# The down projection of a hybrid decoder trunk: seven-product steps spread anew, table load moved to its beginning, residual a step later, tail in program order

## The chip, the cores and the metric

The kernel runs on one core of one Trainium2 chip. The metric is the time of one execution on the device in microseconds (us); lower is better. Every kernel is run several times, and the median is what is compared. A profile is one further execution, recorded by the hardware profiler.

The core's engines work side by side, each through its own queue in order: TensorE (PE in the profile; PEld is its loading of the stationary operand), VectorE (DVE), ScalarE (ACT), GpSimd (POOL) and SyncE (SP), which here issues nearly all DMA transfers. Engines wait for each other through semaphores. Matrix products add into PSUM, where VectorE and ScalarE read them.

## The reference, cut to what matters

The model is one layer over 256 tokens with 2048 channels: two token mixers, cross-attention, and a feed-forward part, all in float32. Only the feed-forward part's second matrix and the final norm are touched:

```
def conv_glu_ffn(u, w_up, conv_w, conv_b, w_down):
    gate, up = jnp.split(u @ w_up, 2, axis=-1)
    gate = causal_dwconv(gate, conv_w, conv_b)
    return (jax.nn.gelu(gate, approximate=False) * up) @ w_down
...
        h = h + conv_glu_ffn(u, ffn_w_up[l], ffn_conv_w[l], ffn_conv_b[l], ffn_w_down[l])
    return rms_norm(h, final_norm_g)
```

Here `w_down` is 5632 x 2048, and `rms_norm` divides each token by the root of the mean square of its 2048 channels and multiplies by a gain per channel.

## The kernel before, in words

**Precision.** Products run on float32 rounded to a shorter form (`F32R`). To keep full precision every operand is split into a rounded part `hi` and the remainder `lo`, and a product is made of three: hi x hi, hi x lo, lo x hi (`mm_tok`). ScalarE makes `hi` by a cast, VectorE makes `lo` by a subtraction.

**Weights.** All weight tiles (128 x 2048 floats, 1 MB) stand in one list, `order`, in the order of their use. `weights()` hands out the next one and has up to two more started ahead. `issue()` starts one: a DMA on SP into one of three `raw` buffers (L140), then two casts and two subtractions of 1024 columns (L126, L127). The results lie in a ring of five buffers for `hi` and five for `lo`, freed when the products that read them are done.

**The down projection** (from L899 on) works through the 2048 output channels in two halves, `i` = 0 and 1. A half is four blocks of PSUM, `acc[0]` to `acc[3]`: 128 tokens x 512 channels each, b // 2 the tokens and b % 2 the channels. The 5632 hidden channels are taken in 22 steps of 256. `down_steps` gives their order and says of each whether it is ordinary or one of `NST` = 7 that use Strassen's scheme:

- An ordinary step forms 2 x 2 blocks of output from 2 x 2 blocks of input and weights in eight block products, each made of three: 24 matrix products of 512 columns.
- A seven-product step forms seven products of sums and differences, 21 matrix products, four of which go to PSUM blocks of their own (`own`). For it `seven_forms` (L158 to L169) makes sums of the weight blocks on VectorE, in between four pairs of cast and subtraction: L158, L159, then the sums L164, L165 and L166, two more pairs, the sum L169, and a last pair of 512 columns. It fills four ring buffers. `input_forms(s)` (L905 to L921) makes the sums of the input on VectorE (L910, L914), splits three of them into `xs` (the cast L916 on ScalarE, the remainder L917) and one into the place of an input block that is no longer needed (L919, L920). All tiles named `c` share one buffer.

Before the change the order is, in both halves: two ordinary steps and a seven, six times; one ordinary step and a seven; two ordinary steps. The sevens are thus steps 2, 5, 8, 11, 14, 17 and 19 of 0 to 21. `input_forms(s)` is named at step 3 s of the first half.

**The residual** is added on TensorE: at steps 0, 4, 8 and 12 of each half a tile `hr` of the residual (256 KB, from `h2_d`, L976, one buffer) is loaded and multiplied by the identity into `acc`, in eight products of 128 columns.

**After the last seven of a half** the four `own` blocks are joined into a tile in SBUF (the copy on ScalarE at L989 or L991; VectorE at L992 to L995). In the first half that copy stands in a critical section (L987), together with a load of ScalarE's function table that holds logarithm and exponential (L988); the functions before it were Gelu and copies.

**The end of a half** goes block by block: VectorE adds `acc` to the joined tile (L998), ScalarE squares it and sums along the row (L1000), VectorE multiplies by the gain (L1002; the gain tile `gr` is loaded at L939 at the beginning of each half). In the second half the last two steps, both ordinary, are run block by block, and after a token group's second block its four partial sums are reduced: VectorE adds them (L1006), ScalarE makes the reciprocal root by logarithm and exponential (L266, L267), VectorE and ScalarE scale the token group's channels (L1009, L1012, L1014), and three DMAs write them out (L1011, L1013, L1015).

**What sets the order.** The program is written in Python in one order; a scheduler then places the instructions of every engine's queue by a model of their times, earlier-written ones first where several are ready, and adds the semaphores. So an instruction whose data are there early can stand well ahead of where it is written. `tc.keep_in_program_order` pins an instruction to its written order on its engine, and `tc.tile_critical` keeps a few instructions together as one unit.

Of the kernel before, what the change touches and what calls it, by code (L numbers as in the profile page):

```python
# [9 lines left out]
F32 = mybir.dt.float32  # L10
# [3 lines left out]
AF = mybir.ActivationFunctionType  # L14
# [5 lines left out]
P = 128  # L20
# [29 lines left out]
def down_steps(half):  # L50
    rest = list(range(NST, KF // 2))
    if half:
        rest = rest[-4:] + rest[:-4]
    steps = []
    for s in range(NST):
        steps += [(False, rest.pop(0)) for _ in range(2 if s < NST - 1 else 1)] + [(True, s)]
    return steps + [(False, k) for k in rest]


# [5 lines left out]
def hybrid_trunk(ctx, tc, xT, memT, par, cst, msk, w_k0, w_ka, w_va, w_hg, w_hv, w_ghg, w_bhg, w_dt,  # L65
# [199 lines left out]
    def rsqrt(out, ps, scale, eps_t):  # L265
        S.activation(out=out, in_=ps, func=AF.Ln, bias=eps_t, scale=scale)  # L266
        S.activation(out=out, in_=out, func=AF.Exp, scale=-0.5)  # L267
# [637 lines left out]
    def input_forms(s):  # L905

        k = 2 * s
        tmp = fd.tile([P, 4, 512], F32, name="c")
        a, d = ha[:, k:k + 2, 0:T], ha[:, k:k + 2, T:2 * T]
        V.tensor_tensor(out=tmp[:, 0:2, 0:T], in0=a.bitcast(F32), in1=d.bitcast(F32), op=ALU.add)  # L910
        a11, a21, a12, a22 = [tmp[:, i, j * P:(j + 1) * P] for i in range(2) for j in range(2)]
        y1, x2, x4, y3 = [tmp[:, 2, j * P:(j + 1) * P] for j in range(4)]
        for out, p, q in ((y1, a21, a22), (x2, a11, y1), (x4, a12, x2), (y3, a21, a11)):
            V.tensor_tensor(out=out, in0=p, in1=q, op=ALU.subtract)  # L914
        three = tmp[:, 2, 0:3 * P].rearrange("p (j t) -> p j t", j=3)
        S.copy(out=xs[:, s, :, 0:P], in_=three)  # L916
        V.tensor_tensor(out=xs[:, s, :, P:2 * P], in0=three, in1=xs[:, s, :, 0:P].bitcast(F32),  # L917
                        op=ALU.subtract)
        S.copy(out=ha[:, k, P:T], in_=y3)  # L919
        V.tensor_tensor(out=ha[:, k, T + P:2 * T], in0=y3, in1=ha[:, k, P:T].bitcast(F32),  # L920
                        op=ALU.subtract)  # L921
# [5 lines left out]

    rows = outT.rearrange("(g p) c -> p g c", p=P)
    ss = fd.tile([P, 2, 4], F32, name="ss")
    cs, gr = [], []  # L930
    for i in range(2):
        steps = down_steps(i)
        acc = [pj.tile([P, 512], F32, name="proj") for _ in range(4)]
# [1 line left out]
            + [pm_.tile([P, 512], F32, name="misc") for _ in range(2)]  # L935
        if i:
            acc, own = own, acc
        gr.append(fd.tile([P, 1024], F32, name="gr"))
        nc.sync.dma_start(out=gr[i], in_=fin_g[i:i + 1, :].partition_broadcast(P))  # L939
        for j, (seven, q) in enumerate(steps):  # L940
            last = i == 1 and j >= len(steps) - 2
            if i == 0:
                for s in range(NST):
                    if j == 3 * s:
                        input_forms(s)
            w = weights()
            if last and j < len(steps) - 1:
                held = w, q
# [19 lines left out]
            else:  # L968
                for k in range(2):
                    for b in range(4):  # L970
                        mm_tok(acc[b], inputs(2 * q + k, b // 2), w(2 * k + b % 2, 512),
                               start=j == 0 and k == 0, stop=j == len(steps) - 1 and k == 1)
            if j % 4 == 0 and j < 16:

                hr = fd.tile([P, 2, T], F32, name="hr")
                nc.sync.dma_start(out=hr, in_=h2_d[:, 8 * i + j // 2:8 * i + j // 2 + 2, :])  # L976
# [5 lines left out]
            if seven and q == NST - 1:  # L982
                c = fd.tile([P, 4, 512], F32, name="c") if i == 0 else \
                    big.tile([P, 4, 512], F32, name="h")
                cs.append(c)
                if i == 0:
                    with tc.tile_critical():  # L987
                        nc.scalar.preload_act_table_set("natural_log_exp_and_others")  # L988
                        S.copy(out=c[:, 0, :], in_=own[0])  # L989
                else:  # L990
                    S.copy(out=c[:, 0, :], in_=own[0])  # L991
                V.tensor_tensor(out=c[:, 2, :], in0=own[2], in1=c[:, 0, :], op=ALU.subtract)  # L992
                V.tensor_tensor(out=c[:, 1, :], in0=own[1], in1=c[:, 2, :], op=ALU.add)
                V.tensor_tensor(out=c[:, 2, :], in0=own[3], in1=c[:, 2, :], op=ALU.add)
                V.tensor_tensor(out=c[:, 3, :], in0=own[1], in1=c[:, 2, :], op=ALU.add)  # L995
        for b in range(4):
            g, n = b // 2, b % 2
            V.tensor_tensor(out=c[:, b, :], in0=acc[b], in1=c[:, b, :],  # L998
                            op=ALU.subtract if b == 2 else ALU.add)
            S.activation(out=acc[b], in_=c[:, b, :], func=AF.Square,  # L1000
                         accum_out=ss[:, g, 2 * i + n:2 * i + n + 1])
            V.tensor_tensor(out=c[:, b, :], in0=c[:, b, :], in1=gr[i][:, n * 512:n * 512 + 512],  # L1002
                            op=ALU.mult)
            if i == 1 and n == 1:
                r = fd.tile([P, 2], F32, name="r", bufs=2)
                V.tensor_reduce(out=r[:, 0:1], in_=ss[:, g, :], axis=AX.X, op=ALU.add)  # L1006
                rsqrt(r[:, 1:2], r[:, 0:1], 1.0 / D, eps_t)
                one, two = cs[0][:, 2 * g:2 * g + 2, :], c[:, 2 * g:2 * g + 2, :]
                V.tensor_scalar(out=two[:, 0, :], in0=two[:, 0, :], scalar1=r[:, 1:2], scalar2=None,  # L1009
                                op0=ALU.mult)  # L1010
                nc.sync.dma_start(out=rows[:, g, 1024:1536], in_=two[:, 0, :])  # L1011
                S.activation(out=two[:, 1, :], in_=two[:, 1, :], func=AF.Copy, scale=r[:, 1:2])  # L1012
                nc.scalar.dma_start(out=rows[:, g, 1536:2048], in_=two[:, 1, :])  # L1013
                V.tensor_scalar(out=one, in0=one, scalar1=r[:, 1:2], scalar2=None, op0=ALU.mult)  # L1014
                nc.sync.dma_start(out=rows[:, g, 0:1024].rearrange("p (n c) -> p n c", n=2), in_=one)  # L1015


# [108 lines left out]
```

## Time and profile before

| what | us |
|---|---|
| median of three runs | 2277.38 |
| lowest and highest of them | 2276.11, 2279.4 |
| the profiled execution, its own time | 2275.68 |
| its span, first to last instruction | 2273.9 |
| VectorE busy in the span | 1645.5 |
| ScalarE busy in the span | 1372.4 |

The profile belongs to the execution of 2275.68 us; 1.8 us of it lie outside the span. A row of a view in order of time has the start, the duration, the engine with the line, the operation, the tiles (written <- read), shapes and count, and in brackets the idle time of the engine before it and what ended it. A row of a view by stage has the stage, its length, the busy time of PE, PEld, DVE, ACT and POOL with the number of instructions, the granted TensorE clock, the DMA share and GB/s. In the chain of waits a row has start, length, what, and count. All matrix products carry the line of a helper, L82, so they are told apart by tiles: in the first half `acc` is `proj` and `own` is two `lev` and two `misc`; in the second the two change places.

The down projection lies from about 2024 us to the end of the span. SP's part in it:

```
hr<-h_d SPq DMA_DIRECT2D x8, 256.0 KB, 5.0
gr<-in_fin_g SPq DMA_DIRECT2D x2, 512.0 KB, 3.8
out<-c SPq DMA_DIRECT2D x2, 512.0 KB, 3.2
```

The last number is the median time from issue to landing in us.

### The profile page before, as it was taken

To read this page: it belongs to the slowest core of one execution; us is meant where nothing else is said; L and a number is where in the kernel's file an instruction comes from. 1 tells how busy PE (TensorE), PEld (TensorE's weight loads), DVE (VectorE), ACT (ScalarE), POOL (GpSimd) and SP (SyncE) were. 2 spreads that over 40 slices of the span, in tenths; PEclk is the share of its full clock that TensorE was granted. 3 is DMA by queue.
4 is the path that set the end of the run, shared out by engine and by line. 5 is a ranking of instruction groups with operands and counts; after the bars stand their busy time and mean duration, and the time that the engine had idled before them with its cause. 6 is when DMAs were issued, how large, how long until landed. Compare 5 with 4: busy or idle time off the path is not lost.

```text
span 2273.9 us, 34864 instructions
## 1 busy us (share of the span) xinstructions
PE 2256.7 (99%) x13848; PEld 1964.6 (86%) x13848; DVE 1645.5 (72%) x2718; ACT 1372.4 (60%) x2116; POOL 1.3 (0%) x9
## 2 busy tenths in 40 slices
PE   9999999999999999999999999999999999999998
PEld 8888888888888888888888888888888888888786
DVE  8878879796556677755676755667776777788876
ACT  7566767676446777764556655556555555555544
POOL 0000000000000000000000000000000000000000
PEclk9999999999999999999999999999999999999999
DMA  8645444545555555455565545565555555555563
GB/s 312 236 169 184 167 169 166 182 161 205 186 187 189 187 184 188 168 181 189 186 238 213 199 172 179 178 209 188 190 193 191 185 187 191 194 198 193 196 230 130
DMA packets 70051, 434.90 MB, mean 191 GB/s; under 512 B 7904, under 2 KB 12544, under 8 KB 20864
## 3 DMA queue, kind: packets, MB, share of 16 engines
q1 hardware_dynamic: 69456, 432.09, 53.4%
q8 instruction: 108, 1.77, 0.3%
q10 hardware_dynamic: 432, 0.58, 0.1%
q14 instruction: 55, 0.45, 0.1%
HBM read 426.32 MB, written 6.32 MB: 190 GB/s over the span
## 4 chain that ended last, share of the span: by engine, by line
PE 97%; DVE 1%; ACT 0%; DMA 0%; issue 0%; SPq 0%; DVEq 0%; ACTq 0%
PE proj L82 88%; PE misc L82 5%; PE lev L82 4%; DVE lo L127 0%; DMA raw<-in_w_k 0%; PE lev L686 0%; DVE lo L159 0%; ACT hi L126 0%; DVE e L505 0%; PE lev L802 0%; DVE e L518 0%; ACT L267 0%; ACT L266 0%; DVE s L263 0%; ACT hi L158 0%
## 5 line engine op out<-in xcount | busy, mean ns | idle before, releaser
L82 PE MATMUL proj<-s,hi 128*128 128x512 f32 x4976 | 1196.6, 392 | 2.5 <-ACT hi L343 1.4
L127 DVE TENSOR_TENSOR lo<-raw,hi 128x1024 fp32r<-128x1024 f32 x738 | 884.0, 1222 | 361.9 <-PE proj L82 268.7
L82 PEld LDWEIGHTS proj<-s,hi 128*128 128x128 f32 x4976 | 913.8, 188 | 183.4 <-DVE s L263 2.0
L126 ACT CAST hi<-raw 128x1024 fp32r<-128x1024 f32 x738 | 770.4, 1048 | 421.8 <-PE proj L82 378.9
L82 PEld LDWEIGHTS proj<-s,lo 128*128 128x128 f32 x4976 | 639.5, 191 | 25.0
L82 PE MATMUL proj<-s,lo 128*128 128x256 f32 x4976 | 647.7, 283 | 0.0
L82 PE MATMUL proj<-hi,s 128*128 128x512 f32 x682 | 216.9, 391 | 0.0
L247 ACT COPY jt<-proj 128x256 f32<-128x256 f32 x263 | 97.5, 371 | 152.7 <-PE proj L82 152.0
L82 PEld LDWEIGHTS proj<-hi,s 128*128 128x128 f32 x682 | 127.8, 188 | 26.3
L82 PE MATMUL proj<-lo,s 128*128 128x512 f32 x341 | 132.8, 389 | 0.0
L158 ACT CAST hi<-raw 128x1024 fp32r<-128x1024 f32 (+1 forms) x56 | 51.6, 943 | 80.3 <-DVE raw L166 49.3
L881 DVE SCALAR_TENSOR_TENSOR gc<-g,par_t,gc 128x255 f32<-128x255 f32 x88 | 42.7, 485 | 55.0 <-ACT gc L879 53.4
L159 DVE TENSOR_TENSOR lo<-raw,hi 128x1024 fp32r<-128x1024 f32 (+1 forms) x56 | 60.0, 1090 | 26.6 <-ACT hi L158 26.2
L82 PEld LDWEIGHTS proj<-lo,s 128*128 128x128 f32 x341 | 64.1, 188 | 12.6
L649 DVE SCALAR_TENSOR_TENSOR sz<-t,par_t,sz 128x255 f32<-128x255 f32 (+2 forms) x96 | 46.2, 481 | 19.9 <-ACT sz L646 18.5
L258 DVE SCALAR_TENSOR_TENSOR s<-h,par_t,s 128x256 fp32r<-128x256 f32 x32 | 15.5, 485 | 36.8 <-ACT s L257 36.6
L253 ACT COPY jt<-proj 128x256 f32<-128x256 f32 x32 | 11.9, 372 | 47.0 <-DVE h L252 47.0
L726 ACT ACTIVATE gs<-r 128x256 f32<-128x256 f32 x32 | 13.4, 419 | 39.5 <-DVE r L248 39.5
L82 PE MATMUL proj<-hi,ha 128*128 128x512 f32 x104 | 36.2, 392 | 0.5 <-ACT hi L158 0.5
L518 DVE TENSOR_TENSOR e<-e,kq 128x256 f32<-128x256 f32 x96 | 34.2, 420 | 0.0
L505 DVE TENSOR_TENSOR e<-bb 128x256 f32<-128x256 f32 x96 | 33.6, 421 | 0.4
L82 PE MATMUL lev<-hi,s 128*128 128x512 f32 x92 | 32.7, 390 | 0.0
(287 smaller groups left out, 1759.2 us busy)
## 6 DMA issues: line engine op xcount, KB each, us to landing
raw<-in_w_up SPq DMA_DIRECT2D x88, 1024.0 KB, 4.8
raw<-in_w_hg SPq DMA_DIRECT2D x48, 1024.0 KB, 4.8
raw<-in_w_m SPq DMA_DIRECT2D x48, 1024.0 KB, 4.8
raw<-in_w_dn SPq DMA_DIRECT2D x44, 1024.0 KB, 4.8
raw<-in_w_hv SPq DMA_DIRECT2D x16, 1024.0 KB, 4.8
raw<-in_w_ghg SPq DMA_DIRECT2D x16, 1024.0 KB, 4.8
raw<-in_w_bhg SPq DMA_DIRECT2D x16, 1024.0 KB, 4.8
raw<-in_w_gm SPq DMA_DIRECT2D x16, 1024.0 KB, 4.8
```

The source lines that it names most:

```text
L82: ins = PE.matmul(*args, **kwargs)
L126: S.copy(out=hi[:, c - a:d - a], in_=raw[:, c:d])
L127: V.tensor_tensor(out=lo[:, c - a:d - a], in0=raw[:, c:d], in1=hi[:, c - a:d - a].bitcast(F32), op=ALU.subtract)
L158: S.copy(out=hi[:, 0:d - c], in_=raw[:, c:d])
L159: V.tensor_tensor(out=lo[:, 0:d - c], in0=raw[:, c:d], in1=hi[:, 0:d - c].bitcast(F32), op=ALU.subtract)
L247: S.copy(out=tmp, in_=ps[:, T:2 * T])
L258: V.scalar_tensor_tensor(out=dst[:, T:2 * T], in0=src, scalar=g, in1=dst[:, 0:T].bitcast(F32), op0=ALU.mult, op1=ALU.subtract)
L505: V.tensor_tensor(out=lev[hw].rearrange("p (n c i) -> p n c i", c=2, i=hw), in0=free(bb, 0, [(2 * hw, nb), (T + hw, 2), (1, hw)]), in1=fre ...
L518: V.tensor_tensor(out=ev, in0=ev, in1=free(kq, 0, [(2 * hw, nb), (T + hw, 2), (1, hw)]), op=ALU.mult)
L649: V.scalar_tensor_tensor(out=o[:, s:T], in0=raw[:, 0:T - s], scalar=pc("m2_cw", 4 * c + 3 - s), in1=o[:, s:T], op0=ALU.mult, op1=ALU.add)
L726: S.activation(out=s, in_=z, func=AF.Sigmoid)
L881: V.scalar_tensor_tensor(out=gc[:, s:T], in0=g[:, 0:T - s], scalar=pc("f_cw", 3 * c + 2 - s), in1=gc[:, s:T], op0=ALU.mult, op1=ALU.add)
```

## The change

All of it lies in the down projection.

- `down_steps`: the ordinary steps ahead of the seven sevens are 2, 2, 1, 2, 1, 2, 1 in the first half and 3, 2, 1, 2, 1, 2, 1 in the second. The sevens become steps 2, 5, 7, 10, 12, 15, 17 and 3, 6, 8, 11, 13, 16, 18; four and three ordinary steps follow the last. `input_forms(s)` is named at step 2 s. The weights' layout in memory follows the order.
- The function table is loaded in `input_forms(1)`, in a critical section with the cast L916. The copy after the first half's last seven stands alone.
- The residual comes at steps 1, 5, 9 and 13.
- The gain multiplies of the first half's blocks are named at steps 4 to 7 of the second half. The gain tile is one variable, loaded at step 0 of the first half and step 11 of the second.
- At the end of the second half every instruction of VectorE and ScalarE is pinned to program order; logarithm and exponential are written out there for that, in place of the helper `rsqrt`.

```diff
@@ down_steps
-    for s in range(NST):
-        steps += [(False, rest.pop(0)) for _ in range(2 if s < NST - 1 else 1)] + [(True, s)]
+    for s, ordinary in enumerate((2, 2, 1, 2, 1, 2, 1) if half == 0 else (3, 2, 1, 2, 1, 2, 1)):
+        steps += [(False, rest.pop(0)) for _ in range(ordinary)] + [(True, s)]
@@ input_forms
-        S.copy(out=xs[:, s, :, 0:P], in_=three)
+        if s == 1:
+            with tc.tile_critical():
+                nc.scalar.preload_act_table_set("natural_log_exp_and_others")
+                S.copy(out=xs[:, s, :, 0:P], in_=three)
+        else:
+            S.copy(out=xs[:, s, :, 0:P], in_=three)
@@ before the loop over the halves
-    cs, gr = [], []
+    cs = []
+
+    def gains(c, b):
+        V.tensor_tensor(out=c[:, b, :], in0=c[:, b, :], in1=gr[:, b % 2 * 512:b % 2 * 512 + 512],
+                        op=ALU.mult)
+
+    def follow(ins):
+
+        if i == 1:
+            tc.keep_in_program_order(ins)
+
+    formed = 0
@@ in a half
-        gr.append(fd.tile([P, 1024], F32, name="gr"))
-        nc.sync.dma_start(out=gr[i], in_=fin_g[i:i + 1, :].partition_broadcast(P))
         for j, (seven, q) in enumerate(steps):
+            if j == 11 * i:
+                gr = fd.tile([P, 1024], F32, name="gr")
+                nc.sync.dma_start(out=gr, in_=fin_g[i:i + 1, :].partition_broadcast(P))
+            if i == 1 and 4 <= j < 8:
+                gains(cs[0], j - 4)
...
-                for s in range(NST):
-                    if j == 3 * s:
-                        input_forms(s)
+                if formed < NST and j >= 2 * formed:
+                    input_forms(formed)
+                    formed += 1
...
-            if j % 4 == 0 and j < 16:
+            if j % 4 == 1 and j < 16:
...
-                if i == 0:
-                    with tc.tile_critical():
-                        nc.scalar.preload_act_table_set("natural_log_exp_and_others")
-                        S.copy(out=c[:, 0, :], in_=own[0])
-                else:
-                    S.copy(out=c[:, 0, :], in_=own[0])
+                S.copy(out=c[:, 0, :], in_=own[0])
@@ at the end of a half
-            V.tensor_tensor(out=c[:, b, :], in0=acc[b], in1=c[:, b, :],
-                            op=ALU.subtract if b == 2 else ALU.add)
-            S.activation(out=acc[b], in_=c[:, b, :], func=AF.Square,
-                         accum_out=ss[:, g, 2 * i + n:2 * i + n + 1])
-            V.tensor_tensor(out=c[:, b, :], in0=c[:, b, :], in1=gr[i][:, n * 512:n * 512 + 512],
-                            op=ALU.mult)
-            if i == 1 and n == 1:
+            follow(V.tensor_tensor(out=c[:, b, :], in0=acc[b], in1=c[:, b, :],
+                                   op=ALU.subtract if b == 2 else ALU.add))
+            follow(S.activation(out=acc[b], in_=c[:, b, :], func=AF.Square,
+                                accum_out=ss[:, g, 2 * i + n:2 * i + n + 1]))
+            if i == 0:
+                continue
+            follow(V.tensor_tensor(out=c[:, b, :], in0=c[:, b, :], in1=gr[:, n * 512:n * 512 + 512],
+                                   op=ALU.mult))
+            if n == 1:
                 r = fd.tile([P, 2], F32, name="r", bufs=2)
-                V.tensor_reduce(out=r[:, 0:1], in_=ss[:, g, :], axis=AX.X, op=ALU.add)
-                rsqrt(r[:, 1:2], r[:, 0:1], 1.0 / D, eps_t)
+                follow(V.tensor_reduce(out=r[:, 0:1], in_=ss[:, g, :], axis=AX.X, op=ALU.add))
+                follow(S.activation(out=r[:, 1:2], in_=r[:, 0:1], func=AF.Ln, bias=eps_t, scale=1.0 / D))
+                follow(S.activation(out=r[:, 1:2], in_=r[:, 1:2], func=AF.Exp, scale=-0.5))
...
-                S.activation(out=two[:, 1, :], in_=two[:, 1, :], func=AF.Copy, scale=r[:, 1:2])
+                follow(S.activation(out=two[:, 1, :], in_=two[:, 1, :], func=AF.Copy, scale=r[:, 1:2]))
```

The other two scalings of the tail (L1009, L1014) are pinned in the same way.

More of the change, by code (lines that the diff above doesn't have):

```diff
@@ L1007, in hybrid_trunk @@
-                rsqrt(r[:, 1:2], r[:, 0:1], 1.0 / D, eps_t)
+                follow(V.tensor_reduce(out=r[:, 0:1], in_=ss[:, g, :], axis=AX.X, op=ALU.add))
+                follow(S.activation(out=r[:, 1:2], in_=r[:, 0:1], func=AF.Ln, bias=eps_t, scale=1.0 / D))
+                follow(S.activation(out=r[:, 1:2], in_=r[:, 1:2], func=AF.Exp, scale=-0.5))
                 one, two = cs[0][:, 2 * g:2 * g + 2, :], c[:, 2 * g:2 * g + 2, :]
-                V.tensor_scalar(out=two[:, 0, :], in0=two[:, 0, :], scalar1=r[:, 1:2], scalar2=None,
-                                op0=ALU.mult)
+                follow(V.tensor_scalar(out=two[:, 0, :], in0=two[:, 0, :], scalar1=r[:, 1:2],
+                                       scalar2=None, op0=ALU.mult))
@@ L1011, in hybrid_trunk @@
                 nc.sync.dma_start(out=rows[:, g, 1024:1536], in_=two[:, 0, :])
-                S.activation(out=two[:, 1, :], in_=two[:, 1, :], func=AF.Copy, scale=r[:, 1:2])
+                follow(S.activation(out=two[:, 1, :], in_=two[:, 1, :], func=AF.Copy, scale=r[:, 1:2]))
                 nc.scalar.dma_start(out=rows[:, g, 1536:2048], in_=two[:, 1, :])
-                V.tensor_scalar(out=one, in0=one, scalar1=r[:, 1:2], scalar2=None, op0=ALU.mult)
+                follow(V.tensor_scalar(out=one, in0=one, scalar1=r[:, 1:2], scalar2=None, op0=ALU.mult))
```

## The prediction

> **What bounds the kernel now.** I read the page first, then busy time by stage for the down projection, then its instructions in order of time.
>
> ```profile
> span 2273.9 us, 34864 instructions
> ## 1 busy us (share of the span) xinstructions
> PE 2256.7 (99%) x13848; PEld 1964.6 (86%) x13848; DVE 1645.5 (72%) x2718; ACT 1372.4 (60%) x2116; POOL 1.3 (0%) x9
> ```
> ```profile
> 2037.00:2075.00 38.00, 38.00 (x177) 31.76 (x176) 36.71 (x63) 22.43 (x30) 0.00 (x0) 1.00 0.56 203
> ...
> 2135.40:2264.70 129.30, 129.25 (x585) 106.86 (x584) 100.77 (x112) 63.88 (x78) 0.00 (x0) 1.00 0.51 188
> ```
>
> TensorE is busy 99% of the span, and in most of the down projection all of the time, at a granted clock of 1.00 (the column after the engines). The change moves work about but adds and removes no matrix product. So it can win only where TensorE stands still: at the beginning of the down projection, between its two halves, and after the last product. The first row also shows the danger: VectorE is busy 36.71 of 38.00 us in the early part of the first half.
>
> The pitch of the products is the measure for everything below; the chain of waits gives it.
>
> ```profile
> 2121.29 6.80 PE proj L82 x30
> ```
>
> That is 6.80 / 30 = 0.227 us for a product with 512 columns. An ordinary step has 24 of them (5.44 us), a step with seven products 21 (4.76 us). The two rows about the beginning, and then those between the halves:
>
> ```profile
> 2031.67 0.61 PE L82 MATMUL proj<-hi,ha 128*128 128x512 f32 x2
> 2032.62 0.57 PE L82 MATMUL proj<-cst_t,hr 128*128 128x128 f32 x3 [0.34 <-DVE s L917]
> ```
> ```profile
> 2131.78 0.39 PE L82 MATMUL proj<-hi,ha 128*128 128x512 f32 x1
> 2132.68 0.49 PE L82 MATMUL proj<-hi,ha 128*128 128x512 f32 x1 [0.51 <-ACT hi L158]
> 2133.41 0.50 PE L82 MATMUL proj<-lo,ha 128*128 128x512 f32 x1 [0.23 <-DVE lo L159]
> ...
> 2134.89 0.50 PE L82 MATMUL proj<-lo,h 128*128 128x512 f32 x1 [0.52 <-DVE lo L127]
> 2135.23 0.40 PE L82 MATMUL proj<-hi,h 128*128 128x512 f32 x1
> ```
>
> Two products from 2031.67 should let the next start at 2032.12; it starts at 2032.62, so 0.50 us is lost (gap A). From 2131.78 to 2135.23 there are six pitches (two starts lie in the omitted place), 1.36 us; it takes 3.45, so 2.09 us is lost (gap B).
>
> **The change, part by part.**
>
> *The table load leaves the boundary.* What ScalarE does there:
>
> ```profile
> 2129.87 1.28 ACT L988 ACT_TABLE_LOAD   x1 [2.56 <-DVE raw L169]
> 2131.16 0.59 ACT L989 COPY c<-lev 128x512 f32<-128x512 f32 x1
> 2132.01 0.62 ACT L158 CAST hi<-raw 128x512 fp32r<-128x512 f32 x1 [0.26 <-ACTq L987]
> 2132.53 1.99 ACT L126 CAST hi<-raw 128x1024 fp32r<-128x1024 f32 x2
> ```
> ```profile
> L987 ACTq NOP  x2: 14/14/14, 2128.8 to 2131.8; - x2
> L987 ACTq DRAIN  x1: 1776/1776/1776, 2130.0 to 2130.0; - x1
> ```
>
> The critical section holds ScalarE from 2128.8 to 2131.8, 3.0 us, of which the copy is 0.59 and the load 1.28; the remaining 1.1 us is its entry, which waits for other engines. The casts for the last of the seven products (L158) and for the next ordinary step (L126) queue behind it, and those are the releasers that the three late products name. With a bare copy of 0.59 us they come about 2.4 us sooner, more than the longest single wait. Gap B goes: -2.09 us. The copy stays, so I leave 0.1 us there.
>
> *The table load arrives at the beginning*, in the input forms of the second seven-product step (L916). The rows of that place on ScalarE, VectorE, TensorE and SP, and two landing times:
>
> ```profile
> 2036.11 0.52 ACT L916 CAST s<-c 128x384 fp32r<-128x384 f32 x1
> 2036.99 1.06 ACT L126 CAST hi<-raw 128x1024 fp32r<-128x1024 f32 x1 [0.36 <-PE proj L82]
> ```
> ```profile
> 2038.08 1.22 DVE L127 TENSOR_TENSOR lo<-raw,hi 128x1024 fp32r<-128x1024 f32 x1
> ```
> ```profile
> 2036.79 0.39 PE L82 MATMUL lev<-hi,ha 128*128 128x512 f32 x1
> ```
> ```profile
> 2028.38 5.73 SPq L976 DMA_DIRECT2D hr<-h_d  x2
> 2036.71 0.33 SPq L140 DMA_DIRECT2D raw<-in_w_dn  x1
> ```
> ```profile
> DMA to landing us min/median/max: 2.7/5.0/5.3
> ```
> ```profile
> raw<-in_w_dn SPq DMA_DIRECT2D x40, 1024.0 KB, 4.8
> ```
>
> There the section takes 0.52 + 1.28 + 1.1 = 2.9 us, until 2039.0. The cast behind it, L126, then ends at 2040.1 and its remainder on VectorE (1.22) at 2041.3. TensorE began the first seven-product step at 2036.79; if gap A goes, it does at 2036.29, ends at 2041.05, and needs that remainder one product later, at 2041.28. Cover and cost meet: I take +0.1 us. Below, 0 if the entry finds everything done (1.9 us held, not 2.9); above, +4.3 us, if the entry waits for a weight load (a rival).
>
> A rule of the Trainium skill is weighed here: "ScalarE: Activation LUTs", What ACT_TABLE_LOAD costs, gives 1.28 us for the load and about 1.38 more for a drain on each switch. The 1.28 is this trace's number; the extra drain is not seen, for the copy starts at 2131.16, where the load ends, and the 1.78 us drain runs beside both. By the page the section would be some 1.4 us longer, and the sum below 1.4 us smaller.
>
> *The residual a step later.* Gap A stands before the products with the residual tile. Their releaser is given as L917, but the load of that tile, issued at 2028.38 with 2.7 to 5.3 us to landing (2031.1 to 2033.7), fits as well. A step later is 5.44 us of slack, above what is missing either way: -0.50 us. Its DMA may now be issued behind one more weight load on SP; one step hides that. If gap A only moves to the next wait, 0.
>
> *The steps spread anew.* Before, a pair of ordinary steps stands ahead of each seven but the last; now three times in each half a single one does. The forms of a seven are heavy on VectorE, and how near they come shows in the seven of step 8, first half (first remainder, last remainder, first product), and at the one place of the second half where a single ordinary step stood between two sevens (the next step's three remainders, and the product that needs the first):
>
> ```profile
> 2060.35 1.22 DVE L159 TENSOR_TENSOR lo<-raw,hi 128x1024 fp32r<-128x1024 f32 x1
> ...
> 2069.85 0.69 DVE L159 TENSOR_TENSOR lo<-raw,hi 128x512 fp32r<-128x512 f32 x1
> ```
> ```profile
> 2068.98 0.39 PE L82 MATMUL lev<-hi,ha 128*128 128x512 f32 x1
> ```
> ```profile
> 2252.18 3.49 DVE L127 TENSOR_TENSOR lo<-raw,hi 128x1024 fp32r<-128x1024 f32 x3
> ```
> ```profile
> 2253.64 0.40 PE L82 MATMUL lev<-lo,s 128*128 128x512 f32 x1
> ```
>
> The last remainder is ready at 2070.54 and needed 19 products after 2068.98, at 2073.29: 2.75 us of slack. Without one ordinary step TensorE arrives 5.44 us earlier and VectorE has two remainders (2 x 3.49 / 3 = 2.3 us) less to do: the slack becomes 2.75 - 5.44 + 2.3 = -0.4. I take +0.5 us for the first pair of the first half, where the input forms fill VectorE. For the other five: in the second half the remainder was ready at 2252.18 + 1.22 = 2253.40, needed at 2253.64, so such a place just holds, with 0.24 us; I take 0.1 us each, +0.5. Bounds: 0, and the price in the slow rival. The input forms themselves are already pulled ahead as their data allow, so naming them every second step costs nothing new.
>
> *Gain multiplies and their loads.* Four multiplies of the first half leave the boundary for steps 4 to 7 of the second; the second gain load goes from step 0 to step 11, where SP no longer stands before the weights. TensorE does not stop at either place (second row of the stages), so 0; if VectorE is full there, four multiplies at most are late, inside the pairs' bound.
>
> *The tail in program order.* After the last product:
>
> ```profile
> 2266.35 1.29 DVE L1002 TENSOR_TENSOR h<-h,gr 128x512 f32<-128x512 f32 x2
> 2267.55 0.15 DVE L1006 TENSOR_REDUCE r<-ss 128x1 f32<-128x4 f32 x1
> ```
> ```profile
> 2265.95 0.19 ACT L1000 ACTIVATION_READ_ACCUMULATOR misc<-h 128x1 f32 x1
> 2267.74 0.29 ACT L266 ACTIVATE r<-r,eps_t 128x1 f32<-128x1 f32 x1 [1.60 <-DVE r L1006]
> ```
> ```profile
> 2269.48 0.33 SPq L1015 DMA_DIRECT2D out<-c  x1
> ```
>
> The sum of squares is read at 2266.14, but its reduction (L1006) starts at 2267.55, since older scalings and two multiplies stand ahead of it on VectorE. In program order only one multiply does, during the square. With 0.04 us for the handover the reduction starts 1.37 us sooner, and all behind it up to the last output's issue. The first tokens' scalings now stand ahead of the next block's addition on VectorE; that costs nothing as long as they end before that block's products do. -1.37 us; bounds 0, and -1.4 if the handover takes nothing.
>
> The sum: -0.50 - 2.09 + 0.1 + 0.1 + 0.5 + 0.5 - 1.37 = -2.76, say -2.8 us. The profiled execution took 2275.68 us, 1.7 under the median of 2277.38, so it would take 2272.9 and the median becomes 2274.6.
>
> **The rivals.**
>
> 1. Every cover holds: -0.50 - 2.09 - 1.37 = -3.96, 2273.4 us. For it: no stop of TensorE in the second half but the last place. Against: the 2.75 us that the first pair uses up.
> 2. The load's section waits at its entry for a weight load in flight. The load of 2036.71 lands 4.8 us later, at 2041.5; then load, copy, cast and remainder (1.28 + 0.52 + 1.06 + 1.22) end at 2045.6, 4.3 past the need. In place of the 0.1 us above that makes -2.8 - 0.1 + 4.3 = +1.4, 2278.8 us. Against: L916 stands at 2036.11, 0.6 us ahead of that issue.
> 3. Slower: VectorE can't feed the pairs. A seven's forms took 2060.35 to 2070.54, 10.2 us; with 2.3 for the single ordinary step, 12.5 against 10.2 of TensorE, up to 2.3 us lost in each of six pairs, 13.8 in all. It turns the change into a loss from 0.66 us a pair (3.96 / 6); at 1.6 the time is -3.96 + 9.6 = +5.6, 2283 us. For it: 36.71 of 38.00. Against: part of these 10.2 us is input forms, done ahead, and between pairs two ordinary steps give time back.
> 4. The change doesn't do what it says in the tail: pinned order only makes VectorE wait for ScalarE, and the reduction stays late. -2.8 + 1.37 = -1.4, 2276.0 us.
> 5. The drain is paid in series: 1.78 us more at the section, -2.8 + 1.7 = -1.1, 2276.3 us. This is the page's rule above; the copy's start speaks against it.
>
> **How the numbers follow.** The forecast gets 0.40, the rivals 0.25, 0.12, 0.10, 0.08 and 0.05. A measurement tells 0.2%, 4.55 us, from no change: the bounds are 2272.8 and 2281.9. Faster needs the first rival and over half a microsecond of luck between runs: 0.10. Slower is the third, with a little of the second: 0.11. The rest, 0.79, is within. The range runs from 2272.4 (all gains and about 1 us of the spread that the three runs show) to 2279.6 (the second rival with as much); it leaves out the third and the far ends.
>
> **What would show it.** Gap B and the load at L988 gone, no TensorE idle time before the residual products, the last reduction right behind the last read of the sum, and the last output's issue some 1.4 us nearer to the last product. Against it: a TensorE wait on L126 or L127 in the first 20 us of the down projection above 1 us (section), or waits on L159 or L127 repeated at the pairs (VectorE).

## The result, and the profile after

The changed kernel takes 2281.85 us (median of 22 runs, 2280.01 to 2283.18), the kernel before in runs alongside it 2276.9 us (22 runs, 2275.1 to 2279.4): the ratio is 1.0022, 95% interval 1.0016 to 1.0029. It is 5 us slower, where 2.8 us faster was forecast, and lies above the range. The profiled execution took 2281.86 us.

The head of the page of the changed kernel, which answers to the one quoted in the prediction:

```profile
span 2280.1 us, 34865 instructions
## 1 busy us (share of the span) xinstructions
PE 2260.3 (99%) x13848; PEld 1968.2 (86%) x13848; DVE 1644.8 (72%) x2718; ACT 1370.4 (60%) x2116; POOL 1.2 (0%) x9
```

The products are as many as before and the engines' busy times nearly the same. So the time has to be looked for where TensorE waits or runs slowly. The busy time of the changed kernel's stages, same columns as in the prediction:

```profile
2037.50:2042.90 5.40, 0.22 (x1) 0.00 (x1) 1.24 (x2) 1.97 (x3) 0.00 (x0) 0.80 0.68 243
2042.90:2047.60 4.70, 4.67 (x11) 3.73 (x12) 2.67 (x4) 1.46 (x2) 0.00 (x0) 0.50 0.01 3
```
```profile
2047.60:2100.00 52.40, 52.40 (x240) 43.66 (x240) 47.50 (x75) 26.54 (x35) 0.00 (x0) 1.00 0.51 191
2100.00:2132.00 32.00, 31.88 (x144) 25.95 (x143) 25.49 (x28) 18.05 (x20) 0.00 (x0) 1.00 0.53 198
2132.00:2265.40 133.40, 133.33 (x604) 110.66 (x604) 101.32 (x109) 63.18 (x73) 0.00 (x0) 1.00 0.53 193
```

From 2037.5 to 2042.9 us TensorE does next to nothing; in the stage behind it it makes 11 products in 4.70 us, at a granted clock of 0.50. After that it is busy through the rest of the down projection but for some tenths of a microsecond: the place of gap B (behind the last seven of the first half, which the prediction calls the boundary between the halves) cost 2.1 us before; it falls inside the fourth row, and that stage lacks 0.12 us. The products around the stop, in order of time:

```profile
2037.34 0.39 PE L82 MATMUL lev<-hi,ha 128*128 128x512 f32 x1
2042.93 0.76 PE L82 MATMUL proj<-hi,s 128*128 128x512 f32 x1 [5.21 <-ACTq L917]
2043.49 0.63 PE L82 MATMUL proj<-lo,s 128*128 128x512 f32 x1
2043.92 0.63 PE L82 MATMUL proj<-hi,s 128*128 128x512 f32 x1
...
2047.69 0.40 PE L82 MATMUL misc<-hi,ha 128*128 128x512 f32 x1
2047.93 0.39 PE L82 MATMUL proj<-hi,ha 128*128 128x512 f32 x1
```

The stop lies inside the first seven-product step: its first product (`lev`, the block a11) has run, its second (`proj`, from the input form in the tile `xs`, called `s` here) waits for L917, the critical section. From 2037.34 to 2042.93 one pitch of 0.227 is due, so 5.36 us are lost. Then 12 pitches take 5.00 us from 2042.93 to 2047.93 instead of 2.72: 2.28 us more. That is 7.6 us at one place.

ScalarE and SP of the changed kernel at that place, and the rows of the section's lines (durations in ns, lowest, median and highest, then the first and the last start; L1139 is the line that opens the whole program, and six of its eight waits belong to the section's entry, two to the program's end). The last row is the time to landing of the residual loads:

```profile
2036.43 1.04 ACT L126 CAST hi<-raw 128x1024 fp32r<-128x1024 f32 x1
2037.38 0.29 ACT L924 CAST ha<-c 128x128 fp32r<-128x128 f32 x1
2040.87 1.28 ACT L918 ACT_TABLE_LOAD   x1 [3.19 <-issue]
2042.16 0.51 ACT L919 CAST s<-c 128x384 fp32r<-128x384 f32 x1
```
```profile
2037.06 0.33 SPq L995 DMA_DIRECT2D hr<-h_d  x1
```
```profile
L917 ACTq NOP  x2: 14/14/14, 2036.9 to 2042.8; - x2
```
```profile
L1139 ACTq EVENT_SEMAPHORE  x8: 17/38/3270, 2037.0 to 2280.0; - x8
```
```profile
DMA to landing us min/median/max: 2.6/3.5/4.6
```

The section goes from 2036.9 to 2042.8, 5.9 us (between the halves it had been 3.0). Its entry is a row of waits in ScalarE's queue, each for two semaphores. Of the six under L1139 the first, from 2037.0, takes 3.27 us, until 2040.29; the others take some 0.04 us each. In flight is the second residual load, issued at 2037.06, 2.6 to 4.6 us from landing; the trace has it landing at 2040.26, on one of the two semaphores of that wait. Before the change it was issued at 2033.8 (the second of the two that the prediction quotes from 2028.38); there is one buffer for the residual, it comes free with the products that use it, and the change has put these products a step later.

The rest is as the trace of before is read: gap A is gone, gap B is gone, and short stops behind three of the single ordinary steps add up to 0.9 us (0.11 before). The tail comes below.

The time from the first product of the down projection to the issue of the last output is 245.09 us before and 250.61 after, 5.5 us more: -0.5 (gap A), -2.1 (gap B), +7.6 (section), +0.8 (short stops), -0.2 (tail), together +5.6. What else differs between two spans, some 0.7 us here, lies ahead of the changed part.

### The profile page after: what moved, and what is told of

Its sections match the earlier page's. It is cut to its first block, busy times and chain, and to the rows that moved or that the text cites. A ratio compares the mean times of both kernels' runs of the same rounds, so it can differ in the third digit from the quotient of the medians.

```text
span 2280.1 us, 34865 instructions
## 1 busy us (share of the span) xinstructions
PE 2260.3 (99%) x13848; PEld 1968.2 (86%) x13848; DVE 1644.8 (72%) x2718; ACT 1370.4 (60%) x2116; POOL 1.2 (0%) x9
```

## The experiments

Each was run beside the kernel before, whose median was 2276.65 to 2277.07 us in those runs. The last column is the stretch from the first product of the down projection to the issue of the last output, from the trace.

| kernel | median us | ratio to before (95%) | stretch us |
|---|---|---|---|
| before | 2276.9 | | 245.09 |
| changed | 2281.85 | 1.0022 (1.0016 to 1.0029) | 250.61 |
| two residual buffers | 2281.31 | 1.0020 (1.0011 to 1.0028) | 250.22 |
| section with a tile of its own | 2277.52 | 1.0005 (0.9996 to 1.0014) | 246.91 |
| section at the last up block | 2279.49 | 1.0013 (1.0005 to 1.0022) | 247.95 |
| tail not pinned | 2281.12 | 1.0020 (1.0011 to 1.0029) | 251.05 |
| residual back at step 0 | 2278.11 | 1.0005 (0.9996 to 1.0014) | 247.47 |
| plain load, no section | 2274.42 | 0.9991 (0.9983 to 1.0000) | 243.81 |
| before, plain load | 2273.85 | 0.9986 (0.9977 to 0.9995) | 242.32 |
| before, new steps alone | 2278.88 | 1.0007 (0.9999 to 1.0016) | 247.95 |
| built from the findings | 2273.20 | 0.9982 (0.9973 to 0.9991) | 242.02 |
| the same, one more swap | 2272.63 | 0.9982 (0.9973 to 0.9990) | 241.03 |

The first question was what makes the section cost 7.6 us: the load it waits for, the tile it shares, or ScalarE's time.

**Two buffers for the residual.**

```diff
-                hr = fd.tile([P, 2, T], F32, name="hr")
+                hr = fd.tile([P, 2, T], F32, name="hr", bufs=2)
```

> The changed kernel with two buffers for the residual tile instead of one. Theory 1 (the critical section's entry waits for the second residual load, which is issued only when the residual products, now a step later, have freed the one buffer; and TensorE's second product of the first seven-product step waits for the section's end): the load is issued some 7 us sooner, the entry no longer waits 3.27 us for it, the section ends about 3.2 us sooner, TensorE stands still some 2.1 us instead of 5.4 and, being idle for a shorter time, keeps its clock, so the 2.5 us of slow products go too: 5.7 us less than the changed kernel, about 2276. Theory 2 (the new order of the steps starves TensorE and the section only happens to lie there): no more than 0.5 us of difference, about 2281.5.

Measured: 2281.31 us, next to no change, and TensorE stops for 5.5 us as before. As the expectation was put, that speaks for theory 2. The trace says why it does not: the second load is early now, but the scheduler has moved the third one ahead, into the same place (three loads in one row of SP from 2028.14, the last at about 2036, landing at 2039.44), and the entry waits for that one. ScalarE in this run:

```profile
2040.09 1.28 ACT L918 ACT_TABLE_LOAD   x1 [3.32 <-DMA hr<-h_d]
```

Here the row names the load itself. The edit did not take the wait away, so it could not tell the theories apart.

**A tile of its own for the section.**

```diff
-            with tc.tile_critical():
-                nc.scalar.preload_act_table_set("natural_log_exp_and_others")
-                S.copy(out=xs[:, s, :, 0:P], in_=three)
+            own_t = fd.tile([P, 1], F32, name="own_t")
+            with tc.tile_critical():
+                nc.scalar.preload_act_table_set("natural_log_exp_and_others")
+                S.copy(out=own_t, in_=three[:, 0, 0:1])
```

The cast into `xs` stands ahead of it for all `s`.

> The changed kernel, but the critical section holds the table load and a copy of one element per partition into a tile of its own; the cast into xs stands before it, outside. Theory 1, with the wait of TensorE due to the shared tile xs alone: ScalarE is held as long as before (some 6 us), but TensorE goes on; it loses at most 0.6 us when the second half of the next ordinary step's weights is cast late: 7.3 us less than the changed kernel, about 2274.6. If holding ScalarE were what costs: 5 us or more of the 7.9 us stay, 2279 or above. Theory 2: no difference.

Measured: 2277.52 us, 4.3 less than the changed kernel. The section still holds ScalarE until after its load at 2039.63 us, but TensorE no longer stops there:

```profile
2039.63 1.28 ACT L920 ACT_TABLE_LOAD   x1 [2.91 <-issue]
2040.93 0.19 ACT L921 COPY own_t<-c 128x1 f32<-128x1 f32 x1
2041.31 2.95 ACT L126 CAST hi<-raw 128x1024 fp32r<-128x1024 f32 x3 [0.19 <-ACTq L919]
```
```profile
PE proj L82 <- DVE lo L127: 0.8, 2, 0.5
PE proj L82 <- DVE lo L159: 0.5, 2, 0.3
```

The second answer is TensorE's list of waits from 2036 to 2072 us in this run (who waited for whom: us in total, times, the longest): none on the section, several short ones on VectorE's remainders, which are late because the casts are. All gaps between products together make 4.7 us. So the long stop came from the shared tile: TensorE reads the part of `xs` for the first seven, the section writes that for the second, and still the product waits for the section's end. Of the 7.3 us expected 4.3 came; the short stops were put too low.

**The residual back at step 0**, which takes the load out of the section's way:

```diff
-            if j % 4 == 1 and j < 16:
+            if j % 4 == 0 and j < 16:
```

> The changed kernel with the residual back at steps 0, 4, 8 and 12; everything else, the critical section at the beginning too, as changed. Theory 1 (the section's entry waits for the residual load that the later residual products have put off): the second load is issued about 3.3 us sooner, has landed when the section begins, and the section ends about 3 us sooner; TensorE stops for some 2 us instead of 5.4 and keeps its full clock, gap A of 0.5 us returns and VectorE, with less time given to it, leaves 1 to 2 us of short stops at the single ordinary steps. In all 3 to 4.5 us less than the changed kernel: 2277.3 to 2278.8. If the section costs that much whatever is in flight: less than 1.5 us of difference, 2280.4 or above.

Measured: 2278.11 us, 3.7 less than the changed kernel, inside theory 1's range (in the stretch it is 3.1 less, for the short stops add up to 2.8 us, where 1 to 2 were expected). ScalarE, TensorE, and the entry's waits:

```profile
2037.16 1.28 ACT L918 ACT_TABLE_LOAD   x1 [1.20 <-PE proj L82]
```
```profile
2037.22 0.39 PE L82 MATMUL lev<-hi,ha 128*128 128x512 f32 x1
2039.22 0.47 PE L82 MATMUL proj<-hi,s 128*128 128x512 f32 x1 [1.61 <-ACTq L917]
2039.52 0.39 PE L82 MATMUL proj<-lo,s 128*128 128x512 f32 x1
```
```profile
L1139 ACTq EVENT_SEMAPHORE  x8: 17/38/438, 2036.1 to 2276.1; - x8
```

The longest of the entry's waits is 0.44 us instead of 3.27, the section ends 3.7 us sooner, TensorE loses 1.8 us instead of 5.4, and the products behind run at the full pitch. Two edits that look independent are not: the later residual is what makes the section long. And even the short section stops TensorE. Before its residual products TensorE waits 0.5 us again, and in this trace the releaser given is the load `hr`, not L917. The landing times say the same: the load lands at 2032.44 here and at 2032.49 before the change, and the residual products start some 0.13 us behind it in both. Gap A was the load, as the prediction took it.

**The load as a plain instruction.** No section; the table load is pinned to program order instead:

```diff
-            with tc.tile_critical():
-                nc.scalar.preload_act_table_set("natural_log_exp_and_others")
-                S.copy(out=xs[:, s, :, 0:P], in_=three)
-        else:
-            S.copy(out=xs[:, s, :, 0:P], in_=three)
+            tc.keep_in_program_order(nc.scalar.preload_act_table_set("natural_log_exp_and_others"))
+        S.copy(out=xs[:, s, :, 0:P], in_=three)
```

> The changed kernel with the table load as a plain instruction of ScalarE, pinned to program order, and no critical section. Theory 1 (the section is what costs, by its entry's waits and by whatever waits for its end, and the 1.28 us load by itself costs nothing): the stop of 5.4 us and the slow products after it are gone. But that stop also gave VectorE time; as in the run with a tile of its own, 3.5 us of short stops at the places with a single ordinary step come up. 4.5 us less than the changed kernel, about 2277.3, and within 1 us of that run. If the load itself held the casts: 1 us or more above that run.

Measured: 2274.42 us, 7.4 less than the changed kernel and 3.1 less than the run with a tile of its own. ScalarE in this run:

```profile
2037.74 1.05 ACT L126 CAST hi<-raw 128x1024 fp32r<-128x1024 f32 x1 [0.35 <-PE proj L82]
2038.82 1.28 ACT L917 ACT_TABLE_LOAD   x1
2040.11 2.00 ACT L126 CAST hi<-raw 128x1024 fp32r<-128x1024 f32 x2
```

The load takes 1.28 us, and the next cast starts where it ends; TensorE loses nothing to it. (The load is written ahead of the cast of `s`, but it stands behind that cast, which starts at 2036.68: the pin did not hold it to its place among instructions that are not pinned.) The whole 7.6 us were the section. The short stops at single ordinary steps are 1.7 us here, 1.5 of them at two places of the first half, such as this one:

```profile
2067.72 0.40 PE L82 MATMUL proj<-hi,s 128*128 128x512 f32 x1
2068.53 0.50 PE L82 MATMUL proj<-lo,s 128*128 128x512 f32 x1 [0.41 <-DVE lo L127]
```

The 3.5 us expected of them were too much; most of those in the run with a tile of its own were due to the section's hold on ScalarE.

**The section ahead, at the last block of the up projection**, and no longer in `input_forms`:

```diff
-        split(hid[c], gc)
+        if c < KF - 1:
+            split(hid[c], gc)
+        else:
+            with tc.tile_critical():
+                nc.scalar.preload_act_table_set("natural_log_exp_and_others")
+                S.copy(out=hid[c][:, 0:T], in_=gc)
+            V.tensor_tensor(out=hid[c][:, T:2 * T], in0=gc, in1=hid[c][:, 0:T].bitcast(F32),
+                            op=ALU.subtract)
```

> The changed kernel with the table load and its critical section moved ahead, to the cast of the last block of the up projection, which only a late step of the down projection reads. Theory 1: ScalarE is idle there for some 2.4 us anyway; the forms of the first seven-product step come up to 3 us later, within their slack; TensorE loses 0 to 0.5 us: 7.6 us less than the changed kernel, about 2274.2. Theory 2: no difference in the early steps, about 2281.5.

Measured: 2279.49 us, 2.4 less than the changed kernel, a third of what was expected. The waits of TensorE from 2024 us on in this run:

```profile
PE proj L82 <- DVE s L924: 1.7, 1, 1.7
PE proj L82 <- DVE lo L127: 0.8, 2, 0.5
PE proj L82 <- DVE lo L159: 0.5, 2, 0.3
```

The section lasts until 2034.4 us there, and the loads of the gain and residual tiles start only then (2035 instead of 2028 us). The stop of 1.7 us stands before the residual products: their load lands at 2039.54 and they start at 2039.67, so it is that load, as in gap A, though the row names L924. VectorE is held up too: it is busy 3.6 of the 8.0 us from 2028, where it is 7.7 in the changed kernel, and the short stops at single ordinary steps add up to 3.8 us instead of 0.9. Why the loads wait for the section was not tested. A section costs at each of the three places where it was tried, each time through something else.

**Before, with a plain load between the halves**: the same replacement in the kernel before, at the copy after the last seven.

> The kernel before with one edit: the table load between the halves is a plain instruction pinned to program order, with no critical section. Theory 1 (gap B is the section's entry and length, not the load or the copy): gap B of 2.1 us goes, 2274.7, ratio 0.9991. If the load of 1.28 us were the cause of gap B: more than half of it stays, ratio 0.9996 or above.

Measured: 2273.85 us, ratio 0.9986 (0.9977 to 0.9995). No gap is left at the boundary: gap B goes with the section. What the load alone would cost at the old place this run does not show, for the scheduler put it at 2134.34 us, behind the four casts, while the copy ahead of which it is written starts at 2129.16. Of the 2.8 us in the stretch 2.1 are gap B and 0.5 the tail (4.74 us from the last product's start to the last output's issue, 5.22 before), whose order the scheduler chose differently.

**Before, with the new order of the steps alone.**

```diff
-    for s in range(NST):
-        steps += [(False, rest.pop(0)) for _ in range(2 if s < NST - 1 else 1)] + [(True, s)]
+    for s, ordinary in enumerate((2, 2, 1, 2, 1, 2, 1) if half == 0 else (3, 2, 1, 2, 1, 2, 1)):
+        steps += [(False, rest.pop(0)) for _ in range(ordinary)] + [(True, s)]
```

The input forms are named at step 2 s, as in the changed kernel, since the new order needs them by then.

> The kernel before with the new order of the steps alone (and the input forms named as early as it needs). Theory 1 with the rival of the pairs: VectorE falls behind in the first half at the single ordinary steps, 3 to 4 us of short stops, while the section between the halves costs its 2.1 us as before: 2279.7 to 2280.7, ratio 1.0015. If the new order costs nothing (the prediction's 0.2 to 1 us): under 2277.7, ratio below 1.0005.

Measured: 2278.88 us, ratio 1.0007 (0.9999 to 1.0016), between the two forecasts: unclear in time alone. The trace has the stretch 2.9 us longer. Some 0.8 us of it are short stops at single ordinary steps around 2068 us; the larger part is at the section behind the last seven, which costs 4.4 us instead of 2.1:

```profile
2121.00:2125.00 4.00, 2.00 (x7) 0.78 (x5) 2.45 (x4) 3.73 (x6) 0.00 (x0) 1.00 0.21 43
2125.00:2128.40 3.40, 3.37 (x8) 2.73 (x9) 3.40 (x4) 1.64 (x3) 0.00 (x0) 0.50 0.96 354
```

TensorE is busy for half of the first stage, and gets half the clock in the second. Of the 4.4 us 2.7 are stops (2.1 before) and 1.7 are lost at half clock behind them. The stops are longer because the casts behind the section start 0.5 us after TensorE wants the product of the first of them; before they started just as it did. In both orders one ordinary step stands ahead of that seven; why the section comes later against the products was not settled.

**The tail not pinned**: `follow` does nothing.

```diff
-        if i == 1:
-            tc.keep_in_program_order(ins)
+        return
```

> The changed kernel without the pinned order in the tail. Theory 1 about the tail (the gain multiply writes in place and so waits for the square that reads the same tile; in program order the last addition and the last reduction each stand behind such a multiply, so pinning gives back what it wins): the time from the start of the last product to the issue of the last output goes from 5.0 to about 5.2 us, a difference in time of under 0.5 us. The prediction's step (pinning wins 1.4 us): 1.4 us more than the changed kernel, about 2283.2.

Measured: 2281.12 us; the tail from the start of the last product to the last output's issue is 4.86 us without the pin and 4.98 with it, neither the 5.2 expected nor 1.4 us more. Pinning wins nothing. The changed kernel's tail shows why, on VectorE, with the last product and the last output:

```profile
2270.70 0.39 PE L82 MATMUL misc<-hi,s 128*128 128x512 f32 x1
```
```profile
2271.06 0.69 DVE L1018 TENSOR_TENSOR h<-h,gr 128x512 f32<-128x512 f32 x1 [0.79 <-ACT misc L1014]
2271.67 0.68 DVE L1012 TENSOR_TENSOR h<-misc,h 128x512 f32<-128x512 f32 x1
2273.14 0.69 DVE L1018 TENSOR_TENSOR h<-h,gr 128x512 f32<-128x512 f32 x1 [0.79 <-ACT misc L1014]
2273.75 0.15 DVE L1022 TENSOR_REDUCE r<-ss 128x1 f32<-128x4 f32 x1
```
```profile
2275.68 0.33 SPq L1032 DMA_DIRECT2D out<-c  x1
```

The gain multiply (L1018) writes the tile in place that the square on ScalarE reads, so it waits 0.79 us for it each time. In program order the last addition (L1012) stands behind the third block's multiply and starts 0.54 us after the data could be there, and the reduction (L1022) stands behind the fourth block's and starts 0.6 us after the sum is read.

**A version built from the findings**: the old order of the steps, the residual and the gains as changed, the plain load, and the tail pinned in this order on VectorE (a block's square follows its addition on ScalarE):

```
add(0)
gain(0)
add(1)
r0 = root(0)
gain(1)
second(0, r0)
add(2)
write(0, r0)
gain(2)
add(3)
r1 = root(1)
gain(3)
second(1, r1)
write(1, r1)
```

Here `root` is reduction, logarithm and exponential, `second` ScalarE's scaling of a token group and its output, `write` the other two. The expectation speaks of every multiply behind the reduction; in this order that holds for blocks 1 and 3, while those of blocks 0 and 2 stand right behind their additions.

> A version built from what the runs so far point to: the changed kernel with the old order of the steps, the plain pinned table load, and the tail pinned in a new order: each block's gain multiply after the reduction instead of ahead of it, and the third block's addition ahead of the first tokens' scalings. Theory 1: gap A -0.5, gap B -2.1, tail -1.4 (last product to last output's issue 3.8 us instead of 5.2), no stops at pairs: 2272.8, ratio 0.9983. Theory 2 for the tail (it is bound by the chain of addition, square, logarithm, exponential and scaling, whatever the order): 4.8 us or more in the tail, 2274.

Measured: 2273.20 us, ratio 0.9982 (0.9973 to 0.9991); no stop of TensorE but 0.11 us. The tail is 4.80 us, not 3.8. That is the figure of theory 2, but the rows show the last addition still behind a multiply, and the next run tells the two apart:

```profile
2263.31 0.69 DVE L1015 TENSOR_TENSOR h<-h,gr 128x512 f32<-128x512 f32 x1 [0.34 <-ACT misc L1010]
2263.92 0.68 DVE L1008 TENSOR_TENSOR h<-misc,h 128x512 f32<-128x512 f32 x1
2265.40 0.16 DVE L1020 TENSOR_REDUCE r<-ss 128x1 f32<-128x4 f32 x1 [0.79 <-ACT misc L1010]
```

**One more swap** in it: `add(3)` ahead of `gain(2)`.

> The version with the old order of the steps, the plain pinned load and the reordered tail, with one more swap: the last addition stands ahead of the third block's gain multiply. In the run without the swap that multiply waited in place for the square and put the last addition off from 2262.95 to 2263.92. Theory 1 (the waits of VectorE for ScalarE's square, by the in-place multiply, are what the program order of the tail costs): last product to last output's issue 3.8 us instead of 4.8, 1 us less, 2272.2, ratio 0.9978. Theory 2 (the chain itself is as long): no difference, 4.6 us or more.

Measured: the tail is 3.84 us, 0.96 less, as theory 1 has it, and the reduction has the sum 0.19 us after VectorE is free:

```profile
2264.18 0.69 DVE L1008 TENSOR_TENSOR h<-misc,h 128x512 f32<-128x512 f32 x1
2264.78 0.68 DVE L1015 TENSOR_TENSOR h<-h,gr 128x512 f32<-128x512 f32 x1
2265.66 0.16 DVE L1020 TENSOR_REDUCE r<-ss 128x1 f32<-128x4 f32 x1 [0.19 <-ACT misc L1010]
```

The median is 2272.63 us, ratio 0.9982 (0.9973 to 0.9990): faster than both kernels, but the last microsecond is seen in the trace alone; the ratios of the two versions do not differ, and the kernel before with a plain load, one edit, lies within their intervals (0.9986).

## Why the prediction was wrong

The step that failed is "The table load arrives at the beginning", +0.1 us with 4.3 as its upper bound. It cost 7.6. The runs show three things in its place.

- The step reckoned with the casts queued behind the section on ScalarE, and asked when the next ordinary step needs them. The one that waits is TensorE itself, for the section's end, because the section writes the tile `xs` that it reads; with another tile that wait is gone. The trace of before could not show it (there the section wrote a tile that no product reads), but the code could: the tile is named in the section and in the seven-product step.
- The second rival had the entry wait for a weight load in flight. It waited for a load in flight, but the residual's, and the change put it there: "one step hides that" was said of the residual products, without asking who else waits for the load that is issued when they free the buffer. With the residual at step 0 the entry's longest wait is 0.44 us instead of 3.27.
- 2.3 us of the 7.6 are products at half clock after the stop. That a stop of over 5 us has a price behind it was in no term.

The tail, -1.37 us, gave -0.24. The step read that the reduction was late because older work stood ahead of it, which is so, and put it behind one multiply "during the square". That multiply writes in place what the square reads, and can't run during it. The row of before that shows it was there; the idle time ahead of L1002 is ended by L1000:

```profile
2261.67 0.69 DVE L1002 TENSOR_TENSOR h<-h,gr 128x512 f32<-128x512 f32 x1 [0.79 <-ACT lev L1000]
```

In another order, with the third block's multiply behind the last addition and the fourth's behind the reduction, the tail is 1.38 us shorter than before (5.22 to 3.84), the size that was forecast.

Right were gap A (-0.5) and gap B (-2.1, and by its own cause: without the section in the kernel before it is gone). The steps spread anew were forecast to cost 1.0 us; short stops of 0.8 us more than before were measured in the changed kernel, 1.6 more with the plain load. That the first lies near the forecast is in part luck: the long stop gave VectorE time, and in the three runs with a section where that stop is shorter or gone the short stops come to 2.8 (residual at step 0), 3.8 (last up block) and 4.7 us (a tile of its own). With what was measured in place of the terms, -0.5 - 2.1 + 7.6 + 0.8 - 0.2 = +5.6, where the stretch is 5.5 us longer; the medians moved by 5.0.

On the rule of the Trainium skill about the table load ("ScalarE: Activation LUTs", What ACT_TABLE_LOAD costs): the plain load of this case takes 1.28 us, the cast behind it starts 0.01 us later with no drain between, and the measurement decides here.

Open is why TensorE waits for a section that writes another part of the tile: that it is the whole tile that counts in a section is read from the one run with a tile of its own, and other splits of `xs` were not tried. Outside a section the parts are told apart: in the run with the plain load TensorE starts on the first seven's part at 2036.86 us, while the cast into the second's (2036.68 to 2037.19) still runs. Nor was every edit of the change run by itself; the gain multiplies' new place shows no stop in any trace, and was not priced.

## What to carry to other kernels

A critical section is an entry barrier for its engine: price it by the loads that are in flight at its place in the schedule and by every reader of the tiles it writes, and use a pinned plain instruction where one does (and look in the trace where the scheduler put it). A step that is moved takes its buffer with it: ask which load waits for the buffer, and who waits for that load. An in-place operation waits for the other readers of its tile, so in a tail put it behind whatever the end hangs on.

## What the runs showed of the hardware

- Behind a stop of 5.4 us TensorE ran 4.7 us at a granted clock of 0.50, a pitch of 0.43 us a product; behind one of 1.8 us it kept the full clock. But a long stop is not needed: in the run with the new steps alone three stops of 1.2, 0.5 and 0.9 us, in a stretch of 4.0 us with 2.00 us of work, were followed by 3.4 us at 0.50. "TensorE: Matmul & The Clock Gate" of the Trainium skill, Part 1, tells of a free-running window of 3.4 us whose busyness sets the clock; the 3.4 us agree. How much work such a window must hold the runs do not settle; the 3.4 us ahead of the drop in the second case (2121.6 to 2125.0) held 1.46 us.
- A function table load that is not in a section took 1.28 us of ScalarE and nothing else (the row at 2038.82 us of the run with the plain load); inside a section the same load stood in a stretch of held ScalarE of 3.0 us (the kernel before), 5.9 us (the changed kernel) and 4.7 us (the section at the last up block, 2029.6 to 2034.4).
